# A decoder trunk with mLSTM, differential attention and grouped experts on one core: negated attention scores, maps mixed in one operation, pinned additions

## The chip, the cores and the metric

The kernel runs on one core of a Trainium2 chip. The metric is the device time in microseconds (us). Five engines work from queues of their own, each in order: TensorE (PE in the profile; PEld its weight loads), VectorE (DVE), ScalarE (ACT), GpSimd (POOL) and SyncE (SP), which issues nearly all transfers. Time before: 1250.63 us, median of 3 runs (1246.63 to 1251.24).

## The reference, cut to what matters

512 tokens of 1024 channels pass two layers. Each has a token mixer and then 16 experts in 4 groups, two experts for a token. Layer 0 mixes by an mLSTM, layer 1 by differential attention, which the change touches:

```python
q = _partial_rope(_rms(q, q_norm), positions)      # 8 heads, 2 maps each, 64 dims
k = _partial_rope(_rms(k, k_norm), positions)
q = jnp.transpose(q, (0, 2, 3, 1, 4)) * (B_HEAD_DIM ** -0.5)     # 1/8
...
    sc = jnp.einsum('bhcqd,bhckd->bhcqk', q[:, :, :, s0:e], k[:, :, :, :e])
    mask = (s0 + jnp.arange(Q_BLOCK))[:, None] >= jnp.arange(e)[None, :]
    p = jax.nn.softmax(jnp.where(mask, sc, -jnp.inf), axis=-1)
    a = p[:, :, 0] - lam * p[:, :, 1]
    outs.append(jnp.einsum('bhqk,bhkv->bhqv', a, v[:, :, :e]))
```

## The kernel before, in words

Tokens are worked in four tiles of 128 rows; `xt[t]` keeps tile t of the residual in SBUF through both layers. A layer is a mixer, an output projection, a routing and an expert stage. Large weights come by SP transfers into a few raw buffers (`load`, L212), and are split into a high and a low part: ScalarE copies the high part (L224), VectorE or GpSimd subtracts it (L225); TensorE then makes three products for one.

The order of instructions is not all written by hand. `later` and `step` (L89, L98) put small pieces of work between the products of a projection, so many steps after they become possible. Then a scheduler of the framework sets each engine's final order by its own estimate, except where `ordered` (keep in program order) or `issue_after` binds it.

*Attention, layer 1.* The projection of q, k and v runs in four groups of two heads. `evac_qk` (L839) normalises and rotates a tile of q or k on VectorE, with the reciprocal root on GpSimd (L326), and turns it by TensorE into `qTb` or `kTb`, where the copy on ScalarE scales each channel by `wcq` or `wck` (L863). `scores` (L867) treats one query tile j of one head h; there are 4 x 8 of these, of 128, 256, 384 or 512 columns. For each of its two maps TensorE multiplies (L876), VectorE adds the mask, writes the result to SBUF and reduces its maximum (L879), VectorE scales that maximum by -1/8 (L882), and ScalarE takes the exponential with it as bias and sums the row (L883). Then VectorE takes the reciprocals of both sums (L886), forms the second map's factor (L887), multiplies the second map by it (L888) and adds it to the first (L889). `probs_T` and `values` turn the mixed map and multiply it by v. Beside this the modulation of later stages is computed: ScalarE scales weight rows (L255) and GpSimd accumulates them (L256).

*From layer 0 to layer 1.* The last expert of layer 0 adds its result to the residual out of PSUM banks, two halves for each of the four token tiles (L1575). Layer 1 begins with `normed_T` (L329): for each tile the sum of squares on ScalarE (L332), its scaling on VectorE (L325, the tile `r`), the root on GpSimd, and turning on TensorE.

*Experts.* The experts' weights, 6 transfers of 1 MB for each expert, are prefetched into slots (`Prefetch`, L1238), of which some are buffers that attention used; a slot comes free when the product that reads it is done.

Of the kernel before, what the change touches and what calls it, by code (L numbers as in the profile page):

```python
# [15 lines left out]
AF = mybir.ActivationFunctionType  # L16
ALU = mybir.AluOpType
# [4 lines left out]
P = 128  # L22
S = 512
D = 1024
# [3 lines left out]
NEG = -1e30  # L28
# [32 lines left out]
def trunk(ctx, tc, x, c, positions, norm1, norm2, w_ada, b_ada, a_w_in, a_b_if, a_h_norm, a_w_out,  # L61
# [145 lines left out]
        G.iota(slot, pattern=[[1, P]], base=0, channel_multiplier=0, **ints)  # L207


    loads, last, act_last = [], [], []  # L210

    def load(src, a, n, name, where=None, after=None):  # L212
        pool, tag, bufs = where or (raws, "raw", N_RAW)
# [115 lines left out]
    def normed_T(l, t, pool, junk, dst, rows, bank):  # L329

        ss = small.tile([P, 1], F32, tag="ss", name=f"ss{l}{t}", bufs=4)
        A.activation(junk, xt[t], AF.Square, accum_out=ss)  # L332
        r = rstd_of(ss, 1, D, f"r{l}{t}")
        ps = [bank(f"hT{l}{t}{hf}") for hf in range(2)]
        for kt in range(NK):
            T.transpose(ps[kt // 4][:, kt % 4 * P:(kt % 4 + 1) * P], xt[t][:, kt * P:(kt + 1) * P], ident)
        row = rows[t // 2][:, t % 2 * P:(t % 2 + 1) * P]
        T.transpose(row, r.to_broadcast([P, P]), ident)
        rrow = pool.tile([P, P], F32, tag="rot", name=f"rrows{l}{t}", bufs=2)
        A.activation(rrow, row, AF.Copy)  # L340
        for hf in range(2):
            V.tensor_tensor(dst[:, hf * 4:hf * 4 + 4], ps[hf].rearrange("p (k t) -> p k t", k=4),
                            rrow[:, None, :].to_broadcast([P, 4, P]), op=ALU.mult)
# [425 lines left out]
    def attention_constants(pool):  # L769
# [17 lines left out]
        for nm, w in (("q", b_q_norm), ("k", b_k_norm)):  # L787
            wr = pool.tile([P, R2], F32, name=f"wr{nm}")
            hold(wr[:, 0:1])
            SP.dma_start(wr, w[0:1, 0:R2].to_broadcast([P, R2]))  # L790
            wc = const.tile([P, 1], F32, name=f"wc{nm}")
            hold(wc)
            V.memset(wc, 1.0)
            for c0 in (0, BHD):
                SP.dma_start(wc[c0 + R2:c0 + BHD], w[0:1, R2:].rearrange("o d -> d o"))
            tab = const.tile([P, NT, 2 * R2], F32, name=f"tab{nm}")
            bc = lambda a: a[:, None, :].to_broadcast([P, NT, ROPE_HALF])
            V.tensor_tensor(tab[:, :, 0:8], cos, bc(wr[:, 0:8]), op=ALU.mult)
            V.tensor_tensor(tab[:, :, 8:16], cos, bc(wr[:, 8:16]), op=ALU.mult)
            V.tensor_tensor(tab[:, :, 24:32], sin, bc(wr[:, 0:8]), op=ALU.mult)  # L800
            V.tensor_tensor(tab[:, :, 16:24], sin, bc(wr[:, 8:16]), op=ALU.mult)
            V.tensor_scalar(tab[:, :, 16:24], tab[:, :, 16:24], -1.0, None, op0=ALU.mult)
            tabs.append(tab)
            wcol.append(wc)
        att.extend((nlam, onr))

    def attention(outer, mods):
# [4 lines left out]
        with ExitStack() as st:  # L812
# [10 lines left out]
            maskW = pool.tile([P, S], F32, name="maskW")  # L823
            G.memset(maskW[:, 0:S - P], 0.0)
            past(maskW[:, S - P:])
            V.tensor_scalar(maskW[:, S - P:], maskW[:, S - P:], 0.0, NEG, op0=ALU.is_gt, op1=ALU.mult)
            a1 = scale_of(1, slice(0, 4)) + scale_of(1, slice(4, 8))
            rows = [y_tile(f"rrow1{i}") for i in range(2)]
            for t in range(NT):
# [37 lines left out]
            def scores(j, h):  # L867
                take("mx", 4)
                take("p0", 3)
                n = (j + 1) * P  # L870
                pr = []
                mx = pool.tile([P, 6], F32, tag="mx", name=f"mx{j}{h}", bufs=4)
                for cc in range(2):
                    q0 = cc * BHD
                    ps = y_tile(f"s{j}{h}{cc}")
                    T.matmul(ps[:, 0:n], part(qTs, h)[q0:q0 + BHD, j * P:(j + 1) * P], part(kTs, h)[q0:q0 + BHD, 0:n],  # L876
                             start=True, stop=True)
                    p = pool.tile([P, S], F32, tag=f"p{cc}", name=f"p{j}{h}{cc}", bufs=3)
                    V.tensor_tensor_reduce(p[:, 0:n], ps[:, 0:n], maskW[:, S - n:S], scale=1.0, scalar=NEG,  # L879
                                           op0=ALU.add, op1=ALU.max, accum_out=mx[:, cc:cc + 1])  # L880
                    pr.append(p)
                    V.tensor_scalar(mx[:, cc:cc + 1], mx[:, cc:cc + 1], -0.125, None, op0=ALU.mult)  # L882
                    A.activation(p[:, 0:n], p[:, 0:n], AF.Exp, scale=0.125, bias=mx[:, cc:cc + 1],  # L883
                                 accum_out=mx[:, 2 + cc:3 + cc])
                p0, p1 = pr
                V.reciprocal(mx[:, 4:6], mx[:, 2:4])  # L886
                V.scalar_tensor_tensor(mx[:, 5:6], mx[:, 5:6], mx[:, 2:3], nlam, op0=ALU.mult, op1=ALU.mult)  # L887
                V.tensor_scalar(p1[:, 0:n], p1[:, 0:n], mx[:, 5:6], None, op0=ALU.mult)  # L888
                V.tensor_tensor(p0[:, 0:n], p0[:, 0:n], p1[:, 0:n], op=ALU.add)  # L889
                later(5, lambda: probs_T(j, h, p0, mx))  # L890

            def probs_T(j, h, p0, mx):
# [369 lines left out]
    def moe(l, pool, grow, fetch, by_rank, xgs, lst, lstd, ids, gates, rows2, twins, count, exc, past, pk, eid):  # L1262
# [269 lines left out]
        for e in range(NE):  # L1532
# [32 lines left out]
            if e == NE - 1:  # L1565
                mine = weighted_few(py, e), mine
                for t in range(NT):
# [4 lines left out]
                    to_tokens(banks[t], t, *mine, False, True)  # L1572
                    for hf in range(2):
                        x = xt[t][:, hf * 512:(hf + 1) * 512]
                        V.tensor_tensor(x, x, banks[t][hf], op=ALU.add)  # L1575
            elif e >= NE - NSEL:
                selected.append((weighted_few(py, e), places(e)))
            elif e == NE - NSEL - 1:
# [91 lines left out]
```

## Time and profile before

| | |
|---|---|
| time, median of 3 runs | 1250.63 us |
| the profiled execution: its time | 1244.82 us |
| its span, first to last instruction | 1243.0 us |
| TensorE busy | 1128.2 us, 91% |
| VectorE busy | 855.2 us, 69% |
| ScalarE busy | 686.7 us, 55% |
| GpSimd busy | 378.7 us, 30% |
| granted TensorE clock, mean of the span | 0.939 of full speed |
| chain that ended last, by engine | PE 63%, DVE 18%, DMA 10%, ACT 3%, issue 2%, POOL 2% |

A row of the profile names the line, the engine, the operation, the tile written and those read, the shapes, the count, the busy time and the mean of one in ns, then the idle time of the engine just before it and what ended that. The chain is followed back from the last instruction, at each step to what released it. In a timeline a row begins with its start and its length in us; a row with a count merges instructions that follow each other.

### The profile page before, as it was taken

To read this page: it belongs to the slowest core of one execution; us is meant where nothing else is said; L and a number is where in the kernel's file an instruction comes from. 1 tells how busy PE (TensorE), PEld (TensorE's weight loads), DVE (VectorE), ACT (ScalarE), POOL (GpSimd) and SP (SyncE) were. 2 spreads that over 40 slices of the span, in tenths; PEclk is the share of its full clock that TensorE was granted. 3 is DMA by queue.
4 is the path that set the end of the run, shared out by engine and by line. 5 is a ranking of instruction groups with operands and counts; after the bars stand their busy time and mean duration, and the time that the engine had idled before them with its cause. 6 is when DMAs were issued, how large, how long until landed. Compare 5 with 4: busy or idle time off the path is not lost.

```text
span 1243.0 us, 17100 instructions
## 1 busy us (share of the span) xinstructions
PE 1128.2 (91%) x5826; PEld 824.4 (66%) x5826; DVE 855.2 (69%) x1608; ACT 686.7 (55%) x1146; POOL 378.7 (30%) x273
## 2 busy tenths in 40 slices
PE   6999999997999999977889889988897999999976
PEld 3677777776787774323888768766576787774322
DVE  4566878887899892035867788985767898893024
ACT  3456675443788883104666557655553788883100
POOL 2555481543211111103441554642233211101100
PEclk8999999996999999999899899897796999999998
DMA  9788661284899999996332434310365899999994
GB/s 349 253 287 306 243 209 72 115 325 180 305 388 392 378 382 378 396 413 239 103 136 69 136 113 159 136 69 14 156 269 186 294 390 377 383 379 367 395 413 168
DMA packets 104170, 320.78 MB, mean 258 GB/s; under 512 B 12673, under 2 KB 25097, under 8 KB 103056
## 3 DMA queue, kind: packets, MB, share of 16 engines
q1 hardware_dynamic: 95120, 298.67, 64.8%
q0 software_dynamic: 8960, 20.99, 4.7%
q8 instruction: 47, 0.77, 0.2%
q14 instruction: 43, 0.35, 0.1%
HBM read 309.66 MB, written 20.97 MB: 266 GB/s over the span
## 4 chain that ended last, share of the span: by engine, by line
PE 63%; DVE 18%; DMA 10%; ACT 3%; issue 2%; POOL 2%; SPq 0%; DVEq 0%; POOLq 0%; ACTq 0%
PE pge L233 8%; PE pue L233 8%; PE pge L1298 7%; PE po L233 6%; PE py0e L233 4%; DMA ada<-in_w_ada_dram 4%; PE py1e L233 4%; DMA we<-in_moe_w_gu_dram 3%; PE pye L1325 3%; PE s L876 2%; DMA b00w<-in_b_w_in_dram 2%; PE xTe L386 1%; PE o L908 1%; DVE qrow L856 1%; PE pcf L1357 1%
## 5 line engine op out<-in xcount | busy, mean ns | idle before, releaser
L256 POOL TENSOR_TENSOR acc<-acc,ada 128x1024 f32<-128x1024 f32 x58 | 152.0, 2621 | 68.6 <-ACT ada L255 30.6
L1298 PE MATMUL pge<-we,xfe 128*64 128x512 f32 x448 | 106.9, 619 | 19.3 <-DMA we<-in_moe_w_gu_dram 19.3
L1270 POOL DMA_INDIRECT xg<-h2d,lstd x26 | 26.5, 1018 | 225.1 <-PE xTe L386 154.5
L1307 DVE TENSOR_TENSOR acte<-acte,pge 128x256 f32<-128x256 f32 x14 | 5.9, 421 | 119.9 <-ACT acte L1306 119.9
L255 ACT ACTIVATE ada<-ada,cact 128x1024 f32<-128x1024 f32 x58 | 64.7, 1145 | 37.3 <-DMA ada<-in_w_ada_dram 37.2
L1298 PEld LDWEIGHTS pge<-we,xfe 128*64 128x64 f32 x448 | 30.5, 141 | 74.8 <-issue 51.4
L326 POOL TENSOR_TENSOR qrs<-qrs,nhalf 128x4 f32<-128x4 f32 x32 | 36.0, 1129 | 81.7 <-DVE qrs L325 62.5
L883 ACT ACTIVATE p<-p,mx 128x128 f32<-128x128 f32 (+3 forms) x64 | 35.5, 556 | 44.1 <-DVE mx L882 44.1
L1325 PE MATMUL pye<-we,aTe 128*64 128x512 f32 x224 | 50.8, 594 | 1.7 <-ACT aTe L1314 1.1
L876 PE MATMUL s<-kTb,qTb 64*128 64x128 f32 (+3 forms) x128 | 44.2, 536 | 7.9 <-DVE mx L879 7.0
L471 POOL TENSOR_TENSOR wo<-wo,grow 128x1024 f32<-128x1024 f32 x16 | 40.1, 2524 | 29.7 <-DVE wos102l L225 14.9
L1306 ACT ACTIVATE acte<-pge 128x256 f32<-128x256 f32 x14 | 5.4, 384 | 74.9 <-PE pge L1298 74.9
L1325 PEld LDWEIGHTS pye<-we,aTe 128*64 128x64 f32 x224 | 15.9, 137 | 33.6 <-issue 30.0
L879 DVE CUSTOM_DVE_ANT_0 p<-s,maskW 128x128 f32<-128x128 f32 (+3 forms) x64 | 29.8, 485 | 10.1 <-PE s L876 7.2
L1422 POOL DMA_INDIRECT yd<-yoe,lstd x12 | 14.7, 1224 | 52.3 <-ACT yoe L1517 51.7
L326 POOL TENSOR_TENSOR ors<-ors,nhalf 128x2 f32<-128x2 f32 (+1 forms) x12 | 11.9, 998 | 56.3 <-DVE ors L325 28.2
L908 PE MATMUL o<-vb,aTs 128*128 128x128 f32 x160 | 27.2, 308 | 1.5 <-ACT o L937 0.8
L386 PE MATMUL xTe<-ident,xg 128*128 128x128 f32 x144 | 23.0, 290 | 5.8 <-POOL we L216 3.3
L1338 POOL DMA_INDIRECT yd<-yo,rows x8 | 8.0, 1001 | 65.7 <-ACT yo L1337 65.4
L908 PEld LDWEIGHTS o<-vb,aTs 128*128 128x128 f32 x160 | 23.8, 217 | 6.2 <-ACT aTs L900 1.9
L1337 ACT ACTIVATE yo<-pye,twins 128x512 f32<-128x512 f32 x8 | 5.5, 687 | 38.9 <-PE pye L1325 38.9
L876 PEld LDWEIGHTS s<-kTb,qTb 64*128 64x128 f32 x128 | 16.0, 203 | 16.2 <-DVE mx L879 8.6
(2546 smaller groups left out, 3932.8 us busy)
## 6 DMA issues: line engine op xcount, KB each, us to landing
we<-in_moe_w_gu_dram SPq DMA_DIRECT2D x128, 1024.0 KB, 8.8
we<-in_moe_w_down_dram SPq DMA_DIRECT2D x64, 1024.0 KB, 8.8
ada<-in_w_ada_dram SPq DMA_DIRECT2D x48, 1024.0 KB, 5.5
we<-yd SPq DMA_DIRECT2D x8, 1024.0 KB, 18.3
wo<-in_a_w_out_dram SPq DMA_DIRECT2D x4, 1024.0 KB, 5.0
wo<-in_b_w_out_dram SPq DMA_DIRECT2D x4, 1024.0 KB, 4.9
x<-in_x_dram SPq DMA_DIRECT2D x4, 512.0 KB, 4.6
qk0w<-in_a_w_in_dram SPq DMA_DIRECT2D x2, 1024.0 KB, 15.4
```

Of the source, the lines that this page charges most:

```text
L233: T.matmul(ps, (xh, xh, xl)[i], w, start=first and i == 0, stop=last and i == 2)
L255: A.activation(raw[:, k], raw[:, k], AF.Copy, scale=cact[:, kt:kt + 1])
L256: G.tensor_tensor(acc, acc, raw[:, k], op=ALU.add)
L326: pows.append(G.tensor_tensor(r, r, nhalf[:, 0:ncol], op=ALU.pow))
L386: T.transpose(ps[:, k * P:(k + 1) * P], row[:, kt * P:(kt + 1) * P], ident)
L471: G.tensor_tensor(raw[:, k], raw[:, k], grow, op=ALU.mult)
L876: T.matmul(ps[:, 0:n], part(qTs, h)[q0:q0 + BHD, j * P:(j + 1) * P], part(kTs, h)[q0:q0 + BHD, 0:n], start=True, stop=True)
L879: V.tensor_tensor_reduce(p[:, 0:n], ps[:, 0:n], maskW[:, S - n:S], scale=1.0, scalar=NEG, op0=ALU.add, op1=ALU.max, accum_out=mx[:, cc:cc ...
L883: A.activation(p[:, 0:n], p[:, 0:n], AF.Exp, scale=0.125, bias=mx[:, cc:cc + 1], accum_out=mx[:, 2 + cc:3 + cc])
L908: T.matmul(po[:, 0:P], aT[:, kb * P:(kb + 1) * P], part(vs, h)[:, kb * P:(kb + 1) * P], start=kb == 0, stop=kb == j)
L1298: T.matmul(pgu[hf * CS:(hf + 1) * CS].rearrange("p (g c) -> p g c", g=2), x[:, kt], w[:, :, hf], start=kt == 0, stop=kt == NK - 1))
L1325: T.matmul(py[hf * CS:(hf + 1) * CS], aT[:, k, ch * CS:(ch + 1) * CS], w[:, 0, hf * 512:(hf + 1) * 512], start=ch + k == 0, stop=ch + k == 2))
```

## The change

q is scaled by -1/8 through `wcq`, once, so that the score products come out as the negated, scaled scores; the mask's constant changes its sign; the reduction takes the minimum, which is the bias of the exponential as it stands, and the exponential has the scale -1. L882 goes. The two operations that mix the maps become one. The last additions of a layer are kept in program order, and in layer 1 the scaling `r` of tiles 2 and 3 is issued after the last of layer 0's additions.

```diff
@@ normed_T
-        r = rstd_of(ss, 1, D, f"r{l}{t}")
+        with tc.issue_after(added[0].ins) if added and t > 1 else nullcontext():
+            r = rstd_of(ss, 1, D, f"r{l}{t}")
@@ attention_constants
+            if nm == "q":
+                V.tensor_scalar(wc, wc, -0.125, None, op0=ALU.mult)
@@ attention
-            V.tensor_scalar(maskW[:, S - P:], maskW[:, S - P:], 0.0, NEG, op0=ALU.is_gt, op1=ALU.mult)
+            V.tensor_scalar(maskW[:, S - P:], maskW[:, S - P:], 0.0, -NEG, op0=ALU.is_gt, op1=ALU.mult)
@@ scores
-                    V.tensor_tensor_reduce(p[:, 0:n], ps[:, 0:n], maskW[:, S - n:S], scale=1.0, scalar=NEG,
-                                           op0=ALU.add, op1=ALU.max, accum_out=mx[:, cc:cc + 1])
+                    V.tensor_tensor_reduce(p[:, 0:n], ps[:, 0:n], maskW[:, S - n:S], scale=1.0, scalar=-NEG,
+                                           op0=ALU.add, op1=ALU.min, accum_out=mx[:, cc:cc + 1])
                     pr.append(p)
-                    V.tensor_scalar(mx[:, cc:cc + 1], mx[:, cc:cc + 1], -0.125, None, op0=ALU.mult)
-                    A.activation(p[:, 0:n], p[:, 0:n], AF.Exp, scale=0.125, bias=mx[:, cc:cc + 1],
+                    A.activation(p[:, 0:n], p[:, 0:n], AF.Exp, scale=-1.0, bias=mx[:, cc:cc + 1],
                                  accum_out=mx[:, 2 + cc:3 + cc])
...
-                V.tensor_scalar(p1[:, 0:n], p1[:, 0:n], mx[:, 5:6], None, op0=ALU.mult)
-                V.tensor_tensor(p0[:, 0:n], p0[:, 0:n], p1[:, 0:n], op=ALU.add)
+                V.scalar_tensor_tensor(p0[:, 0:n], p1[:, 0:n], mx[:, 5:6], p0[:, 0:n], op0=ALU.mult, op1=ALU.add)
@@ moe, the last expert
-                        V.tensor_tensor(x, x, banks[t][hf], op=ALU.add)
+                        added[:] = [V.tensor_tensor(x, x, banks[t][hf], op=ALU.add)]
+                        ordered(added[0])
```

The scheduler works on the whole program, so the order moves at other places too. Two of them matter. The first is VectorE where layer 0 ends, before (x0 to x3 are the token tiles, pcf the banks, r10 to r13 the scalings of layer 1's tiles 0 to 3):

```order
L1575 TENSOR_TENSOR x1_83<-x1_83,pcf11_5042 128x512
L325 TENSOR_SCALAR r10_5134<-ss10_5132 128x1
L325 TENSOR_SCALAR r11_5168<-ss11_5166 128x1
L1575 TENSOR_TENSOR x2_86<-x2_86,pcf20_5075 128x512
L1575 TENSOR_TENSOR x2_86<-x2_86,pcf21_5076 128x512
L325 TENSOR_SCALAR r12_5202<-ss12_5200 128x1
L1575 TENSOR_TENSOR x3_89<-x3_89,pcf30_5085 128x512
L1575 TENSOR_TENSOR x3_89<-x3_89,pcf31_5086 128x512
```

and the same place on VectorE with the change:

```order
L1576 TENSOR_TENSOR x1_83<-x1_83,pcf11_5043 128x512
L325 TENSOR_SCALAR r10_5135<-ss10_5133 128x1
L325 TENSOR_SCALAR r11_5169<-ss11_5167 128x1
L1576 TENSOR_TENSOR x2_86<-x2_86,pcf20_5076 128x512
L1576 TENSOR_TENSOR x2_86<-x2_86,pcf21_5077 128x512
L1576 TENSOR_TENSOR x3_89<-x3_89,pcf30_5086 128x512
L1576 TENSOR_TENSOR x3_89<-x3_89,pcf31_5087 128x512
L325 TENSOR_SCALAR r12_5203<-ss12_5201 128x1
```

The two additions of tile 3 moved ahead of r12. The second is VectorE at head 0, query tile 3, before (p300 and p301 are the two maps, mx30 their column values, qrow and rot belong to the rotation of k):

```order
L879 ISA p301_6267,mx30_6258<-s301_6265,maskW_5118 128x512
L879 ISA mx30_6258 128x1
L855 TENSOR_TENSOR qrow_6202<-qrow_6202,tabk_907 128x4x16
L882 TENSOR_SCALAR mx30_6258<-mx30_6258 128x1
L856 TENSOR_TENSOR qrow_6202<-qrow_6202,rot_6212 128x4x16
L886 RECIPROCAL mx30_6258<-mx30_6258 128x2
L887 SCALAR_TENSOR_TENSOR mx30_6258<-mx30_6258,nlam_873 128x1
L888 TENSOR_SCALAR p301_6267<-p301_6267,mx30_6258 128x512
L889 TENSOR_TENSOR p300_6261<-p300_6261,p301_6267 128x512
```

and VectorE with the change, where the reductions are L882 and the reciprocal is L888:

```order
L882 ISA p301_6249,mx30_6241<-s301_6247,maskW_5119 128x512
L882 ISA mx30_6241 128x1
L888 RECIPROCAL mx30_6241<-mx30_6241 128x2
L889 SCALAR_TENSOR_TENSOR mx30_6241<-mx30_6241,nlam_873 128x1
L890 SCALAR_TENSOR_TENSOR p300_6244<-p301_6249,mx30_6241,p300_6244 128x512
```

The two pieces of rotation moved out from between the reduction and the reciprocal, and the scaling and the multiplication are gone. A reciprocal that has nothing but the reduction's own read-out ahead of it (L882 of the old kernel not counted) stands at 3 of the 32 heads before and at 6 with the change. SP's order is the same in both kernels. On TensorE, ScalarE and GpSimd rows change places within layer 1's beginning, its attention and its output projection, with the same instructions in sum.

## Rows read from the trace of the kernel before

**Rows 1.** The page's first line: span and instructions of the whole execution.

```profile
span 1243.0 us, 17100 instructions
```

**Rows 2.** Stretches: length, busy us (count) of PE, PEld, DVE, ACT, POOL; PEclk, DMA, GB/s.

```profile
636.00:690.00 54.00, 54.00 (x392) 46.42 (x391) 38.68 (x141) 36.74 (x94) 14.44 (x11) 1.00 0.23 79
690.00:760.00 70.00, 60.08 (x405) 50.69 (x403) 59.92 (x134) 42.68 (x102) 42.39 (x21) 0.93 0.44 151
760.00:810.00 50.00, 45.16 (x302) 38.96 (x301) 43.49 (x124) 34.10 (x87) 27.16 (x17) 0.90 0.38 126
810.00:853.00 43.00, 32.80 (x190) 25.47 (x191) 32.18 (x95) 24.75 (x65) 12.72 (x9) 0.83 0.13 50
853.00:900.00 47.00, 42.98 (x189) 31.10 (x187) 33.91 (x81) 23.39 (x65) 17.37 (x9) 0.83 0.29 112
```

**Rows 3.** Chain of waits from 640 to 900 us, shares by line.

```profile
by line: PE s L876 10.0%; issue 5.1%; DVE qrow L856 4.8%; PE o L908 4.2%; DVE p L879 4.1%; PE po L233 4.0%; DVE p L889 3.4%; DVE mod L273 3.4%; DVE qrow L850 3.1%; DVE mx L887 2.5%; DVE p L888 2.3%; PE qkT L862 2.0%; DVE orow L923 1.8%; DVE
```

**Rows 4.** Timeline of all engines from 697 to 705 us.

```profile
697.75 2.49 DVE L888 TENSOR_SCALAR p<-p,mx 128x512 f32<-128x512 f32 x1
...
700.02 5.17 POOL L256 TENSOR_TENSOR acc<-acc,ada 128x1024 f32<-128x1024 f32 x2
700.27 2.71 DVE L889 TENSOR_TENSOR p<-p,p 128x512 f32<-128x512 f32 x1
...
703.32 0.26 DVE L882 TENSOR_SCALAR mx<-mx 128x1 f32<-128x1 f32 x2
...
704.41 0.17 DVE L886 RECIPROCAL mx<-mx 128x2 f32<-128x2 f32 x1 [0.82 <-ACT p L883]
```

**Rows 5.** Groups by line and shape: count | busy us, mean ns | idle before, releaser.

```profile
L882 DVE TENSOR_SCALAR mx<-mx 128x1 f32<-128x1 f32 x64 | 8.5, 146 | 0.2
...
L888 DVE TENSOR_SCALAR p<-p,mx 128x512 f32<-128x512 f32 x8 | 5.9, 734 | 0.2
L888 DVE TENSOR_SCALAR p<-p,mx 128x384 f32<-128x384 f32 x8 | 3.3, 418 | 0.2
L888 DVE TENSOR_SCALAR p<-p,mx 128x256 f32<-128x256 f32 x8 | 2.8, 352 | 0.2
L888 DVE TENSOR_SCALAR p<-p,mx 128x128 f32<-128x128 f32 x8 | 2.3, 283 | 0.2
...
L253 DVE SCALAR_TENSOR_TENSOR acc<-ada,cact,acc 128x1024 f32<-128x1024 f32 x12 | 15.4, 1281 | 11.3 <-DMA ada<-in_w_ada_dram 6.7 <-POOL acc L256 4.6
...
L225 DVE TENSOR_TENSOR b14s0l<-b14w,b14s0h 128x1024 fp32r<-128x1024 f32 x1 | 1.2, 1226 | 3.1 <-ACT b14s0h L224 3.1
...
L879 DVE CUSTOM_DVE_ANT_0 p<-s,maskW 128x512 f32<-128x512 f32 x16 | 10.8, 685 | 3.0 <-PE s L876 2.9
...
L879 DVE CUSTOM_DVE_ANT_0 p<-s,maskW 128x128 f32<-128x128 f32 x16 | 4.1, 283 | 0.9 <-PE s L876 0.7 <-ACT orow L910 0.2
...
L886 DVE RECIPROCAL mx<-mx 128x2 f32<-128x2 f32 x32 | 5.1, 161 | 7.1 <-ACT p L883 6.9
```

**Rows 6.** Timeline where layer 0 ends: start us, us, engine, what.

```profile
573.41 7.14 PE L1357 MATMUL pcf<-yo,self 64*128 64x512 f32 x32 [0.85 <-DVE yo L1331]
...
578.40 1.27 DVE L1575 TENSOR_TENSOR x<-x,pcf 128x512 f32<-128x512 f32 x2
...
581.24 1.15 ACT L255 ACTIVATE ada<-ada,cact 128x1024 f32<-128x1024 f32 x1 [2.94 <-DMA ada<-in_w_ada_dram]
...
583.46 0.15 DVE L325 TENSOR_SCALAR r<-ss 128x1 f32<-128x1 f32 x1 [3.78 <-ACT sq L332]
583.54 1.29 DVE L1575 TENSOR_TENSOR x<-x,pcf 128x512 f32<-128x512 f32 x2
...
584.92 1.06 ACT L332 ACTIVATE sq<-x 128x1024 f32<-128x1024 f32 x1 [1.49 <-DVE x L1575]
```

**Rows 7.** Layer 1's experts: from the timeline of SP, then from the chain.

```profile
938.39 33.84 SPq L218 DMA_DIRECT2D we<-in_moe_w_gu_dram  x4
...
1195.23 20.07 DMA we<-in_moe_w_gu_dram
```

More of the change, by code (lines that the diff above doesn't have):

```diff
@@ L207, in moe_constants @@
         G.iota(slot, pattern=[[1, P]], base=0, channel_multiplier=0, **ints)
-    loads, last, act_last = [], [], []
+    loads, last, act_last, added = [], [], [], []
     def load(src, a, n, name, where=None, after=None):
```

## The prediction

> **What bounds the kernel now.** I read the whole span first, then the stretch in which the edited lines run, then that stretch's chain of waits, then the timeline and the groups of single lines. The profiled execution spans 1243.0 us [rows 1]. The scores, exponentials and mixing of the two maps run in layer 1, from about 640 to 900 us; the additions that are pinned matter at about 575 to 587 us, where layer 0 hands over to layer 1.
>
> The stretch table [rows 2] shows two regimes. From 636 to 690 us TensorE is busy 54.00 of 54.00 us at full clock, and VectorE only 38.68: there a shorter VectorE list buys nothing. From 690 to 853 us VectorE is busy 59.92, 43.49 and 32.18 us of 70, 50 and 43, while TensorE falls to 60.08, 45.16 and 32.80, at a granted clock of 0.93, 0.90 and 0.83 of full speed. Neither is saturated; they wait for one another. From 853 to 900 us it is the same in weaker form.
>
> The chain of waits from 640 to 900 us [rows 3] says how much of an edited line decides the end: the multiplication of the second map (L888) holds 2.3% of 260 us, 6.0 us, the addition of the maps (L889) 3.4%, 8.8 us. L882, the scaling of the maximum, is not among the lines named, the smallest of which holds 1.8%.
>
> The timeline shows why such small operations are on the chain [rows 4]. GpSimd runs accumulations of 2.6 us each (the row at 700.02 holds two), and VectorE operations with operands in SBUF stretch beside them: the 512-column L888 takes 2.49 us and the L889 behind it 2.71. Without a stretch L888 has 283 ns for 128 columns, and 352 for 256 [rows 5].
>
> **The change part by part.**
>
> *The negated scores.* 64 instructions of L882 go. They are busy 8.5 us in sum, 146 ns each, two in a row 0.26 us [rows 4, 5]. Each stands between a reduction and its exponential, so it also delays ScalarE. From the chain the bounds are 0 and 4.7 us (1.8% of 260, the smallest line named) [rows 3]. I take 2.0: it is small work, but in the direct path. The reduction by minimum replaces one by maximum on the same operands; the exponential has another constant scale. Both keep their shapes and counts, and I cost them at nothing. One operation on a 128x1 constant is added, in layer 0's shadow: at most the 0.15 us of an L882, taken as 0.
>
> *The mixing in one operation.* 32 multiplications (L888) go: 5.9 + 3.3 + 2.8 + 2.3 = 14.3 us busy [rows 5]. The 32 additions become operations that multiply by a column and add, of the same width. I take their price as that of the additions: such an operation on 1024 columns, both tensors f32 in SBUF (L253), takes 1281 ns, and a plain subtraction of 1024 columns (L225) 1226 [rows 5]. So what is gained is L888 alone: upper end 14.3, lower end 0 where something else is late, and by the chain 6.0 (42% of 14.3). I take 6.0, since it is read from the stretch itself. Late next where L888 goes are the reciprocal's wait for the exponentials and TensorE's own queue.
>
> [...]
>
> *What moves with it.* With L882 gone, the new order puts the reciprocal directly behind the second reduction in 6 of 32 heads, against 3 before (L882 not counted). VectorE works in order and then idles for the exponentials; one such wait is 0.82 us [rows 4], and all of them now are 6.9 us [rows 5]. Three more cost 2.5 us of VectorE, 42% of it on the path as for L888: +1.0 us. Behind the waiting reciprocal stand the next head's reductions, and behind those TensorE's score products, which need a freed bank. Some TensorE products, POOL accumulations and ScalarE rows change places in this stretch; SP's queue doesn't change. I set no price on that: it has no sign, and the range carries it.
>
> *The pinned additions.* Now the last two additions of layer 0 (token tile 3) stand behind the r of tile 2, which waits for a square on ScalarE that itself stands behind a weight product that waits for a DMA until 581.24. So VectorE, free at 579.67, sits idle until 583.46 and adds tile 3 at 583.54, though TensorE's last bank was written at 573.41 + 7.14 = 580.55 [rows 6]. Pinned ahead, these additions run at about 580.6. The square of tile 3 then needn't wait its 1.49 us before 584.92 [rows 6], and the rows of r copied behind it on ScalarE come as much earlier. The square of tile 2 is not touched: it still waits for the DMA. Gain 1.5, with bounds 0 (the following VectorE work meets a GpSimd accumulation at another moment) and 1.5. The r of tile 2 now waits for the tile 3 additions, at nothing: they end some 1.5 us before its square does. At the end of layer 1 the order is already the pinned one, so nothing comes from there.
>
> *Does it reach the end?* In layer 1's expert stage the weights' transfers set the end: the chain has a weight transfer of 20.07 us at 1195.23, and the queue's last four prefetches wait 33.84 us from 938.39 for slots that only the experts free [rows 7]. So that stream's restart moves with the end of attention, and I carry the gain through one to one.
>
> Sum: 2.0 + 6.0 - 1.0 + 1.5 = 8.5 us. The profiled execution took 1244.82 us, so it would take 1236.3. It lies 5.8 us under the median of the three runs, 1250.63; the same 8.5 us off the median give **1242.1**, 0.7% faster. About 0.5% is what a measurement of this kernel can tell from no change, that is 6.3 us: 1244.4 and 1256.9.
>
> **The rivals.**
>
> *Full relief.* If VectorE alone paces 690 to 900 us, all of L888, and L882 at 4.7, come off, with 2.5 lost to the reciprocals: 14.3 + 4.7 - 2.5 + 1.5 = 18.0, so 1232.6. For it: TensorE's granted clock of 0.83 to 0.93 there, which is low where it has waited. Against: 636 to 690 us can give nothing, and the chain has less than half of L888. Chance 0.17.
>
> *Hidden behind TensorE.* The edits do what they say on VectorE, but the products' own queue is late next, and only the pin and a rest of about 1.5 us remain: 3.0, so 1247.6. For it: TensorE busy 138 of 163 us from 690 to 853. Against: the clock in the same rows. Chance 0.23.
>
> *The mixing at half rate.* [...] Chance 0.05.
>
> *Slower: VectorE's queue stands behind the exponentials.* Each reciprocal that follows its reductions directly stops VectorE for 0.82 us, and with it the next reductions, the score banks and TensorE. Were all 32 heads so placed, 26.2 us of waiting would stand where 6.9 are now: 19.3 more. Fully on the path against 9.5 gained by the rest, that is 9.8 us lost: 1260.4. It decides from 12 more heads on (9.5 / 0.82). For it: a VectorE list without L882 has nothing else to put in between. Against: the order has three more, not twelve. Chance 0.10.
>
> **How the numbers follow.** The forecast keeps 0.45; its own range is 4 to 12 us of gain, 1238 to 1247, by other meetings with GpSimd and the new places on TensorE. Faster by over 0.5% are about four fifths of it and the full relief: 0.36 + 0.17 = 0.53. Slower by over 0.5%: 0.10, and 0.02 for new places that fall badly. The rest, 0.35, is within 0.5%. The range, 1231 to 1251, takes in the forecast, full relief, the hidden case and the half rate, and leaves out the slower one and a tail of the full relief.
>
> **What would show it.** Right: VectorE's busy time from layer 1's scores to their end about 20 us less; the mixing at about what a reduction of its width takes, 0.28 to 0.69 us [rows 5], where it isn't stretched; tile 3's additions right behind tile 2's, with ScalarE's two squares back to back; the reciprocals' wait at about 9 us; TensorE's granted clock from 690 to 853 us higher. Wrong: mixing rows of over 1 us for 512 columns with no GpSimd accumulation beside them (half rate); a reciprocals' wait over 16 us (slower); VectorE that much less busy with TensorE's stretch as long as before (hidden); or a gain that is there when experts of layer 1 begin but not at the end (the transfers hold it).

## The result, and the profile after

| | before | changed |
|---|---|---|
| median of 10 runs each, same batch | 1251.45 us (1246.63 to 1256.41) | 1238.80 us (1235.36 to 1243.24) |
| the profiled execution: its time | 1244.82 us | 1238.19 us |
| its mean granted clock | 0.939 | 0.940 |

The ratio is 0.9895, with a 95% interval of 0.9874 to 0.9917: 13.1 us faster (10.4 to 15.8). The forecast was 8.5 us. The two profiled executions, however, differ by 6.6 us only: the one of the kernel before, 1244.82 us, lies below all ten others. Both figures have to be explained.

The first line of the changed kernel's page, against [rows 1]:

```profile
span 1236.4 us, 17003 instructions
```

The stretch table of the changed kernel, in the stretches of [rows 2] moved 6 us ahead (the same columns):

```profile
630.00:684.00 54.00, 54.00 (x399) 47.45 (x398) 35.91 (x125) 37.52 (x90) 15.98 (x11) 1.00 0.29 98
684.00:754.00 70.00, 64.43 (x424) 55.19 (x424) 57.83 (x120) 44.96 (x110) 40.13 (x22) 0.93 0.41 136
754.00:804.00 50.00, 45.28 (x318) 38.30 (x318) 42.77 (x102) 33.14 (x87) 29.57 (x18) 0.97 0.43 148
804.00:847.00 43.00, 34.63 (x190) 26.48 (x191) 30.16 (x82) 24.86 (x66) 13.13 (x9) 0.78 0.14 50
847.00:894.00 47.00, 42.62 (x190) 32.12 (x190) 30.70 (x64) 24.16 (x67) 17.25 (x9) 0.84 0.29 112
```

TensorE is fuller where it had waited most: 64.43 us of 70 against 60.08, 34.63 of 43 against 32.80. VectorE is a little emptier in each row. The granted clock in these rows is 0.78 to 1.00 of full speed; it is lowest in the row in which TensorE is idle longest, 8.37 us.

To see where the time came from I cut both traces at the same work instead: from the first projection product of the second group's q (`b02p`) to the first of the third group's v (`bv4p`), from there to the first of the fourth group's v (`bv6p`), and on to the end of the last value product. First the kernel before:

```profile
639.40:736.50 97.10, 90.50 (x646) 77.85 (x645) 73.18 (x231) 64.19 (x159) 37.83 (x24) 0.96 0.32 109
736.50:807.50 71.00, 63.27 (x409) 53.00 (x407) 63.39 (x156) 45.05 (x113) 40.78 (x23) 0.90 0.44 149
807.50:903.70 96.20, 80.62 (x412) 60.68 (x412) 69.92 (x186) 51.57 (x140) 32.85 (x20) 0.84 0.20 77
```

and the changed kernel between the same points:

```profile
638.60:736.40 97.80, 93.62 (x645) 79.97 (x644) 70.59 (x192) 64.02 (x159) 35.97 (x22) 0.97 0.32 108
736.40:800.10 63.70, 59.41 (x408) 50.54 (x406) 56.14 (x134) 42.55 (x112) 40.22 (x24) 0.95 0.46 155
800.10:897.00 96.90, 81.86 (x412) 62.41 (x412) 65.83 (x153) 53.37 (x142) 34.87 (x21) 0.82 0.22 84
```

The whole gain of attention in this pair lies in the middle row, 71.0 to 63.7 us, where GpSimd is busiest and VectorE had been busy 63.39 of 71.00. The outer rows are each 0.7 us longer than before, though VectorE lost 2.6 and 4.1 us in them.

The chain of waits of the changed kernel from 638 to 894 us, shares by line, against [rows 3]:

```profile
by line: PE s L879 8.6%; issue 5.0%; PE o L909 3.8%; DVE mx L889 3.8%; PE po L233 3.6%; DVE orow L924 3.4%; DVE qrow L853 3.2%; DVE p L882 3.1%; DVE p L890 2.6%; DVE qrow L858 2.2%; DMA b16w<-in_b_w_in_dram 2.1%; DVE rot L856 2.0%; DVE mod 
```

The two mixing lines held 3.4% and 2.3%, 14.8 us of 260; the one that replaces them (L890) holds 2.6% of 256, 6.7 us. But the factor, a column of one element, rose from 2.5% to 3.8%, and the normalisation of the output rows (L923, now L924) from 1.8% to 3.4%. Part of the time was handed on. The groups say to what. First the rows of the kernel before that [rows 5] doesn't have:

```profile
L887 DVE SCALAR_TENSOR_TENSOR mx<-mx,nlam 128x1 f32<-128x1 f32 x32 | 13.3, 416 | 0.6
...
L889 DVE TENSOR_TENSOR p<-p,p 128x256 f32<-128x256 f32 x8 | 3.4, 422 | 0.1
...
L923 DVE TENSOR_TENSOR orow<-orow,ors 128x512 f32<-128x512 f32 x4 | 2.7, 684 | 0.0
...
L889 DVE TENSOR_TENSOR p<-p,p 128x128 f32<-128x128 f32 x8 | 2.3, 288 | 0.1
```

and the changed kernel:

```profile
L853 DVE TENSOR_TENSOR qrow<-qrow,qrs 128x256 f32<-128x256 f32 x32 | 22.7, 710 | 4.2 <-POOL qrs L326 4.1
L889 DVE SCALAR_TENSOR_TENSOR mx<-mx,nlam 128x1 f32<-128x1 f32 x32 | 14.4, 449 | 0.7
L882 DVE CUSTOM_DVE_ANT_0 p<-s,maskW 128x512 f32<-128x512 f32 x16 | 10.9, 687 | 7.2 <-PE s L879 5.5 <-ACT orow L911 1.6
...
L890 DVE SCALAR_TENSOR_TENSOR p<-p,mx,p 128x512 f32<-128x512 f32 x8 | 8.1, 1019 | 0.2
...
L924 DVE TENSOR_TENSOR orow<-orow,ors 128x512 f32<-128x512 f32 x4 | 6.0, 1500 | 0.0
...
L888 DVE RECIPROCAL mx<-mx 128x2 f32<-128x2 f32 x32 | 5.1, 160 | 7.0 <-ACT p L885 6.6
L890 DVE SCALAR_TENSOR_TENSOR p<-p,mx,p 128x384 f32<-128x384 f32 x8 | 4.9, 615 | 0.1
L890 DVE SCALAR_TENSOR_TENSOR p<-p,mx,p 128x256 f32<-128x256 f32 x8 | 3.9, 483 | 0.2
L890 DVE SCALAR_TENSOR_TENSOR p<-p,mx,p 128x128 f32<-128x128 f32 x8 | 2.8, 348 | 0.2
```

The mixing costs 348, 483 and 615 ns for 128, 256 and 384 columns: 1.04 ns a column, as the addition alone did (288 and 422 ns), and 60 ns more for each operation. The reciprocals' wait for the exponentials is 6.6 us. The reductions of 512 columns wait longer than before, 7.2 against 3.0 us, and mostly for TensorE. L924's four wide rows take 1500 ns on the mean, where they took 684: two of them meet an accumulation and take 1.79 and 2.84 us, and the two others take 0.68 us as before.

What holds VectorE is seen in the changed kernel's timeline near 782 us, VectorE and GpSimd alone:

```profile
781.49 7.47 POOL L256 TENSOR_TENSOR acc<-acc,ada 128x1024 f32<-128x1024 f32 x3 [0.94 <-ACT acc L251]
...
781.67 2.38 DVE L273 TENSOR_TENSOR mod<-cs,vcol 128x8 f32<-128x8 f32 x1
783.97 0.21 DVE L859 TENSOR_TENSOR qrow<-qrow,rot 128x64 f32<-128x64 f32 x1
784.11 0.41 DVE L882 CUSTOM_DVE_ANT_0 p<-s,maskW 128x256 f32<-128x256 f32 x1
...
784.45 2.07 DVE L856 TENSOR_TENSOR rot<-qrow,tabq 128x32 f32<-128x32 f32 x1
...
786.66 2.38 DVE L858 TENSOR_TENSOR qrow<-qrow,tabq 128x64 f32<-128x64 f32 x1
```

Three accumulations, of 2.37 to 2.53 us, run with under 0.1 us between them, and beside each one some VectorE operation is held until it ends, be it of 8, 32 or 64 columns: the accumulations end at 784.02, 786.48 and 788.95 us, the held operations at 784.05, 786.52 and 789.04. The reduction at 784.11, which reads PSUM and SBUF, takes its usual 0.41 (418 ns on the mean of its 16), though the second accumulation starts at 784.10.

The hand-over from layer 0, against [rows 6]:

```profile
579.95 1.28 DVE L1576 TENSOR_TENSOR x<-x,pcf 128x512 f32<-128x512 f32 x2 [0.91 <-PE pcf L1358]
...
580.69 1.15 ACT L255 ACTIVATE ada<-ada,cact 128x1024 f32<-128x1024 f32 x1 [3.04 <-POOL maskW L136]
...
581.75 1.04 ACT L332 ACTIVATE sq<-x 128x1024 f32<-128x1024 f32 x1
...
582.92 1.06 ACT L332 ACTIVATE sq<-x 128x1024 f32<-128x1024 f32 x1
582.92 0.15 DVE L325 TENSOR_SCALAR r<-ss 128x1 f32<-128x1 f32 x1 [1.69 <-ACT sq L332]
```

Tile 3's additions run at 579.95 instead of 583.54, and ScalarE's two squares follow each other without a wait. From the last bank of layer 0 to the first projection product it is 9.38 us instead of 10.75.

And SP's queue in the experts, against [rows 7], from its timeline:

```profile
931.70 34.28 SPq L218 DMA_DIRECT2D we<-in_moe_w_gu_dram  x4
```

It waits about as long as before (33.84 us), from a moment 6.7 us earlier.

| us from the span's start | before | changed | e6_later | e11_before_later |
|---|---|---|---|---|
| first projection product of layer 1 | 591.30 | 589.30 | 587.41 | 587.57 |
| end of the last value product | 903.72 | 896.98 | 894.17 | 899.99 |
| first product of layer 1's experts | 960.59 | 954.51 | 946.88 | 952.79 |
| end | 1243.03 | 1236.40 | 1229.01 | 1235.16 |

### The profile page after: what moved, and what is told of

Read it like the earlier page. It is cut to its first block, busy times and chain, and to the rows that moved or that the text cites. A ratio compares the mean times of both kernels' runs of the same rounds, so it can differ in the third digit from the quotient of the medians.

```text
span 1236.4 us, 17003 instructions
## 1 busy us (share of the span) xinstructions
PE 1127.3 (91%) x5826; PEld 826.3 (67%) x5826; DVE 843.0 (68%) x1513; ACT 685.6 (55%) x1146; POOL 378.4 (31%) x273
## 4 chain that ended last, share of the span: by engine, by line
PE 63%; DVE 16%; DMA 11%; ACT 5%; POOL 3%; issue 2%; SPq 0%; POOLq 0%; DVEq 0%; ACTq 0%
PE pge L233 8%; PE pue L233 8%; PE pge L1299 6%; PE po L233 6%; DMA we<-in_moe_w_gu_dram 5%; DMA ada<-in_w_ada_dram 4%; PE py0e L233 4%; PE py1e L233 4%; PE pye L1326 3%; POOL acc L256 2%; PE s L879 2%; PE pcf L1358 2%; PE xTe L387 1%; ACT ada L255 1%; PE o L909 1%
## 5 line engine op out<-in xcount | busy, mean ns | idle before, releaser
L472 POOL TENSOR_TENSOR wo<-wo,grow 128x1024 f32<-128x1024 f32 x16 | 40.1, 2526 | 33.0 <-DVE wos102l L225 14.3
L882 DVE CUSTOM_DVE_ANT_0 p<-s,maskW 128x128 f32<-128x128 f32 (+3 forms) x64 | 30.0, 485 | 14.4 <-PE s L879 9.7
L909 PEld LDWEIGHTS o<-vb,aTs 128*128 128x128 f32 x160 | 23.5, 212 | 7.7 <-ACT aTs L901 2.1
L326 POOL TENSOR_TENSOR ors<-ors,nhalf 128x2 f32<-128x2 f32 (+1 forms) x12 | 10.8, 901 | 54.4 <-DVE ors L325 42.1
```

Source lines behind the costliest of these rows:

```text
L326: pows.append(G.tensor_tensor(r, r, nhalf[:, 0:ncol], op=ALU.pow))
L472: G.tensor_tensor(raw[:, k], raw[:, k], grow, op=ALU.mult)
L909: T.matmul(po[:, 0:P], aT[:, kb * P:(kb + 1) * P], part(vs, h)[:, kb * P:(kb + 1) * P], start=kb == 0, stop=kb == j)
```

## The experiments

The theory of the prediction, called A below, is that each operation taken away gives the share of it that lay on the path. The main rival, B, is that the new order of the whole list decides, since the scheduler deals VectorE's operations and GpSimd's accumulations out anew for every edit. C is the hand-over, D that VectorE alone paces, E that TensorE's granted clock differs between executions. In us, a ratio is taken of the median before in the same batch: 1249.2 for e1 to e4, 1249.0 for e5 to e8, 1249.1 for e9 to e12. The ratio is not the quotient of the two medians, and the two can differ by 2 or 3 us: by the medians e2_neg gains 8.8 us, and e9_small and e10_wide lose 1.4 and 1.2. The diffs show the lines that matter.

**e1_pin: the pinned additions alone.**

```diff
+        with tc.issue_after(added[0].ins) if added and t > 1 else nullcontext():
+            r = rstd_of(ss, 1, D, f"r{l}{t}")
...
+                        ordered(added[0])
```

> Only the additions are pinned; attention is as before. Theory A (each part gives what it takes off the path): 1.5 us faster than before, all of it between 578 and 587 us, ratio 0.999. Theory B (the new order of instructions, not the work removed, makes the gain): anything from 4 us faster to 4 us slower, since this kernel's attention stage is scheduled anew. Theory C (most of the whole gain of 12.7 us comes from where layer 0 meets layer 1): over 4 us faster.

Measured: 1245.77 us, ratio 0.9981 (0.9956 to 1.0007), 2.4 us, which the runs can't tell from nothing. The trace can: the hand-over takes 8.88 us instead of 10.75, and attention behind it is as long as before (264.2 us against 264.3, from the first `b02p` to the last value product). In all five traces of kernels with the pin the hand-over takes 8.5 to 9.4 us (mean 8.9), in the nine without it 9.9 to 10.9 (mean 10.4). So the pin is worth what was forecast, and C, a gain that comes mostly from there, falls.

**e2_neg: the negated scores alone.**

```diff
-                    V.tensor_scalar(mx[:, cc:cc + 1], mx[:, cc:cc + 1], -0.125, None, op0=ALU.mult)
```

> Only the scores are negated, so that L882 goes; the maps are mixed in two operations, nothing is pinned. Theory A: 2 us faster, ratio 0.998. Theory D (VectorE paces attention, so what it is spared comes off in full and its waits with it): 4.7 to 8.5 us faster, ratio 0.993 to 0.996. Theory B: no fixed sign.

Measured: 1240.45 us, ratio 0.9947 (0.9926 to 0.9969): 6.6 us for 64 operations on one column, three times the term of the forecast. Attention takes 258.5 us.

**e3_mix: the mixing in one operation alone.**

```diff
-                V.tensor_scalar(p1[:, 0:n], p1[:, 0:n], mx[:, 5:6], None, op0=ALU.mult)
-                V.tensor_tensor(p0[:, 0:n], p0[:, 0:n], p1[:, 0:n], op=ALU.add)
+                V.scalar_tensor_tensor(p0[:, 0:n], p1[:, 0:n], mx[:, 5:6], p0[:, 0:n], op0=ALU.mult, op1=ALU.add)
```

> Only the maps are mixed in one operation; L882 stays, nothing is pinned. Theory A: 6.0 us less 2.0 for the operation's 61 ns over a plain addition at 32 heads, so 4 to 6 us faster, ratio 0.995 to 0.997. Theory D: 12 us faster, ratio 0.990. Theory B: no fixed sign.

Measured: 1237.68 us, ratio 0.9922 (0.9890 to 0.9953), 9.7 us. In its profiled execution attention takes 252.9 us at a granted clock of 0.946 there, against 264.3 at 0.903. TensorE is busy for 225.9 us of it, against 234.4 before, with the same products: 8.5 of the 11.4 us lie there, beside the higher clock, and not in waits.

**e4_neg_mix: both, without the pin** (the two diffs above).

> Both changes of attention without the pin. If the parts add up (A or D): the sum of the two single runs, and 1.5 us slower than the whole change, about 11 us faster than before, ratio 0.991. Theory B: it differs from that sum by over 4 us. Theory C: under 9 us faster.

Measured: 1239.91 us, ratio 0.9944 (0.9923 to 0.9965). Both together give 7.0 us, no more than either alone; 16.3 would be their sum. Attention takes 258.3 us, the same as in the changed kernel (258.4). Added prices (theory A in its plain form) fall here. Its median and the change's, 1238.80, are closer than the two ratios, each of which is taken in its own batch.

**e5_before: the kernel before again,** with no edit.

> The kernel before, unchanged, profiled a second time; ratio 1.000. The first profiled execution of before took 1244.8 us, under its median of about 1250. Theory E (TensorE's granted clock in attention makes the difference between executions): the span comes out at 1246 to 1252 us, with the granted clock from the second projection group to the last value product under the 0.903 of the first one and TensorE busy over 235 us there. Rival (the transfers of layer 0 make it): the attention stretch within 1 us of 264.3 again, and layer 0 longer.

Measured: 0.9999 (0.9967 to 1.0031), and a profiled span of 1243.0 us again, at a clock of 0.937. Attention takes 263.3 us, at 0.903 again. So it shows how far two profiles of one kernel agree, 1.0 us here, and decides nothing about E.

**e6_later: the change, with the reciprocals and the mixing put off by one step of the work list.**

```diff
-                p0, p1 = pr
+                later(1, lambda: mixed(j, h, *pr, mx))
+
+            def mixed(j, h, p0, p1, mx):
...
-                later(5, lambda: probs_T(j, h, p0, mx))
+                later(4, lambda: probs_T(j, h, p0, mx))
```

> The whole change, and the reciprocal, the factor and the mixing of each head are put off by one step of the work list, so that other work of VectorE stands between them and the reductions. If the in-order wait of the reciprocal for the exponentials (6.6 us in the profile of the change) is on the path: 3 to 6 us faster than the change, ratio to before 0.985 to 0.987. If it is covered: as the change, 0.990. If one more step of delay makes TensorE wait for the mixed maps at the end of a group: 2 to 5 us slower than the change, 0.992 to 0.994.

Measured: 1227.90 us, ratio 0.9815 (0.9783 to 0.9848). It beats both kernels, by 23.1 us and by about 10 (against e7_dose, which equals the change, in the same batch). But not by the wait that it was aimed at. The groups of e6_later show the reciprocals waiting as long as before, and the factor taking 661 ns on the mean, where it took 449 in the change:

```profile
L892 DVE SCALAR_TENSOR_TENSOR mx<-mx,nlam 128x1 f32<-128x1 f32 x32 | 21.1, 661 | 0.7
...
L891 DVE RECIPROCAL mx<-mx 128x2 f32<-128x2 f32 x32 | 5.1, 160 | 7.1 <-ACT p L885 6.7
```

What moved is the output projection behind attention. Its products of this layer begin at 832.1 us instead of 846.6, between the last heads, and from the last value product to the experts' first product it takes 52.7 us instead of 57.5 (table above). Of the 7.4 us between the two profiled ends 4.8 lie there; 1.9 lie before layer 1's first projection product.

**e7_dose: the change, with 32 multiplications of the second map put back** (by 1.0).

```diff
+                V.tensor_scalar(p1[:, 0:n], p1[:, 0:n], 1.0, None, op0=ALU.mult)
```

> The whole change, and for each head the second map is multiplied by 1.0 in place before the mixing: an operation of the shape of the old L888 comes back (14.3 us of VectorE). Theory A: 6 us slower than the change, ratio to before 0.995. Theory D: 12 to 14 us slower than the change, ratio 1.000. Theory B: no relation to the work put back, 0.988 to 0.992 or over 1.002.

Measured: 1238.09 us, ratio 0.9911 (0.9880 to 0.9941), the same as the change. Its groups show where part of the added work goes:

```profile
L888 DVE RECIPROCAL mx<-mx 128x2 f32<-128x2 f32 x32 | 5.1, 160 | 4.3 <-ACT p L885 3.9
...
L890 DVE TENSOR_SCALAR p<-p 128x256 f32<-128x256 f32 x8 | 4.4, 546 | 0.4 <-ACT p L885 0.4
L890 DVE TENSOR_SCALAR p<-p 128x512 f32<-128x512 f32 x8 | 3.3, 409 | 0.0
L890 DVE TENSOR_SCALAR p<-p 128x384 f32<-128x384 f32 x8 | 2.7, 337 | 0.0
...
L890 DVE TENSOR_SCALAR p<-p 128x128 f32<-128x128 f32 x8 | 1.7, 208 | 0.0
```

The sum of its stretches from the first `b02p` to the last value product, to set beside 258.40 us, TensorE 234.89 and VectorE 192.56 in the changed kernel:

```profile
sum 257.90, PE 233.00 PEld 190.69 DVE 197.15 ACT 160.55 POOL 111.92; mean PE 77.67 PEld 63.56 DVE 65.72 ACT 53.52 POOL 37.31
```

The rows of the 32 added operations last 12.1 us, but VectorE is busy 4.6 us longer only, in part because rows overlap. Its idle time falls by 5.1 us, 2.7 of them from the reciprocals' wait. The granted clock in this stretch is 0.927, against 0.908 in the changed kernel, and TensorE is busy 1.9 us less; so that it is free at an equal clock too is not shown. D, by which it would cost 12 to 14 us, falls.

**e8_mix_pin: the change with L882 kept** (diffs of e1_pin and e3_mix).

> The mixing in one operation and the pin, L882 stays. If parts add up (A, D): slower than the whole change by what L882 is worth, 2 to 6 us, ratio to before 0.992 to 0.994. Theory B, after the run with the mixing alone was ahead of the run with both attention edits (0.9922 against 0.9944): the order without L882 takes back what its work saves, and this kernel is as fast as the whole change or up to 5 us faster, 0.986 to 0.990.

Measured: 1237.69 us, ratio 0.9902 (0.9867 to 0.9937). The negated scores add nothing that shows once the other two parts are in; with six runs, 2 or 3 us would not show.

**e9_small: the kernel before, with L882 doubled.**

```diff
+                    V.tensor_scalar(mx[:, cc:cc + 1], mx[:, cc:cc + 1], 1.0, None, op0=ALU.mult)
```

> The kernel before with the scaling of the maximum doubled: 64 more operations on 128x1, each a multiplication by 1.0 behind L882, 146 ns each, 8.5 us of VectorE in sum. This is the negated scores' saving turned round. Theory A (each operation has its own price on the path; taking L882 away alone gave 0.53%): 6 to 7 us slower, ratio about 1.005, with ScalarE's wait for the reductions about 6 us longer. Theory B (what an edit gives is decided by the new order of the whole list, and not by the work): anything within 8 us on either side, of no fixed sign. The forecast's own term (2.0 us for 64 such operations) would make it 1.0016, that is no difference that can be measured.

Measured: 1250.54 us, ratio 1.0036 (1.0017 to 1.0055), 4.5 us slower (2.1 to 6.9). The timeline of e9_small shows what one costs VectorE's list, L882 being the old and L883 the added one:

```profile
836.49 0.27 DVE L882 TENSOR_SCALAR mx<-mx 128x1 f32<-128x1 f32 x2
836.67 0.27 DVE L883 TENSOR_SCALAR mx<-mx 128x1 f32<-128x1 f32 x2
```

Rows overlap: two of them last 0.27 us, but the next begins after 0.18. So 64 take 5.8 us of the list here, not the 8.5 us of their busy time. The sum of its stretches from the first `b02p` to the last value product, against 264.30 us, TensorE 234.39 and VectorE 206.49 before:

```profile
sum 268.30, PE 239.73 PEld 194.61 DVE 210.64 ACT 160.12 POOL 109.92; mean PE 79.91 PEld 64.87 DVE 70.21 ACT 53.37 POOL 36.64
```

Attention is 4.0 us longer. The length is all in TensorE's busy time, at a granted clock of 0.892 there against 0.903; its idle time is no longer than before (28.6 us against 29.9).

**e10_wide: the kernel before, with the multiplication of the second map doubled.**

```diff
+                V.tensor_scalar(p1[:, 0:n], p1[:, 0:n], 1.0, None, op0=ALU.mult)
```

> The kernel before with the multiplication of the second map doubled: 32 more operations of 128 to 512 columns (by 1.0, in place, ahead of L888), 14.3 us of VectorE in sum. The mixing's saving turned round. Theory A: as much slower as the mixing alone was faster, 0.78%, about 10 us; the forecast's own term says 6.0 us, ratio 1.005. Theory B: not slower in proportion, within 5 us of the kernel before or even faster, as in the change itself, where the same 32 operations put back cost nothing.

Measured: 1250.35 us, ratio 1.0038 (1.0015 to 1.0061), 4.7 us slower (1.9 to 7.6). In its trace attention, on the same terms, is 4.7 us longer:

```profile
sum 269.00, PE 238.64 PEld 193.87 DVE 208.88 ACT 160.04 POOL 114.65; mean PE 79.55 PEld 64.62 DVE 69.63 ACT 53.35 POOL 38.22
```

In the kernel before the added work costs something near the 6.0 us of the forecast; in the changed kernel, e7_dose, it costs nothing that shows. Again TensorE's busy time carries it (238.64 against 234.39 us, clock 0.892).

**e11_before_later: the kernel before, nothing removed, the mixing put off as in e6_later.**

> The kernel before, with nothing removed, and the reciprocals, the factor and the two mixing operations put off by one step of the work list (the turning keeps its place). If putting off is worth the same 0.8% without the change as on top of it (theory B: the place of these operations in VectorE's list counts, not their sum), the ratio is about 0.992 and the time near that of the change. If it only pays once L882 and L888 are gone (theory A, with the reciprocal's wait as what is late next), it is within 0.4% of the kernel before.

Measured: 1240.72 us, ratio 0.9954 (0.9927 to 0.9980), 5.7 us. From the last value product to the experts it takes 52.8 us against 56.9, as in e6_later. So the putting off earns in the same place with and without the change. That is 4.1 of the 7.9 us between the two profiled ends; 3.7 lie before layer 1's first projection product (table above), whose lines this edit does not touch.

**e12_sooner: the kernel before, the same instructions, the turning one step sooner.**

```diff
-                later(5, lambda: probs_T(j, h, p0, mx))
+                later(4, lambda: probs_T(j, h, p0, mx))
```

> A control of how far a new order alone moves the time: the kernel before with the turning of the mixed map put on the work list four steps on instead of five, the same instructions. Theory B: a difference of several us, of either sign, of the size of the single parts' differences (0.2 to 0.8%). Theory A: nothing over 0.3%, since no work is added or taken away, and the mixed map is ready well before.

Measured: 1243.59 us, ratio 0.9973 (0.9947 to 0.9998). A new order with the same work is worth 0.27% here, and in e11 0.46%. Single edits of this kernel can't be priced more finely than that by undoing them one at a time.

**Attention in all fourteen traces** tells the work from the order better than the times do. Taken from the first `b02p` to the last value product, it lasts 261.4 to 264.3 us in the five traces with all of the work (before, e1, e5, e11, e12), 252.9 to 258.7 in the seven that spare some (the change, e2, e3, e4, e6, e7, e8), and 268.2 and 269.1 in the two that add some (e9, e10). The groups don't meet. It isn't the clock alone either: at a granted clock of 0.908 to 0.909 there, e11 takes 263.1 us, and the change, e4 and e6 take 258.4, 258.3 and 258.7. So the work sets the sign in attention, against B in its plain form; but how much is spared doesn't set the size, against A.

**What the clock adds** needs no run of its own. Each execution has its mean granted clock on record. Of the kernel before 86 executions came with e1 to e12: mean 1248.4 us, clock 0.929 to 0.946 of full speed, mean 0.9355. Time and clock go together (correlation -0.82): 0.96 us less for each 0.001. An estimate from 1128.2 us of TensorE work, all of it longer by 0.001 of 0.9355, is near that, 1.2 us. The 15 executions at 0.939 to 0.941 took 1243.4 us on the mean, and the one that was profiled, at 0.939, took 1244.82. The changed kernel's ten executions are all at 0.939 to 0.942, mean 0.9401; the nine up to 0.941 took 1239.2. So at an equal clock the change is worth 4.2 us between means and 6.6 between the two profiles, and the clock, 0.0046 higher, about 4.4 more (an estimate, 0.96 x 4.6). That makes 8.6 of the 13.1 us. By the fitted line instead of the 15 executions the first part is 5.2 and the sum 9.5; the remaining 3.6 us are there because the kernel before, in the batch of the result, took 1251.9 us on the mean, 3.6 over these 86, and the clocks of those ten executions are not on record.

The edits that take work away have mean clocks of 0.9399 to 0.9442, those with equal or more work 0.9349 to 0.9382 (e9_small 0.9360, e10_wide 0.9362). Against the fitted line, that is at an equal clock, e2, e3 and e4 are 3.6, 4.5 and 2.7 us faster, but e1, e12 and e11, which take no work away, are 3.6, 3.1 and 5.1 faster as well, and e9 and e10 2.6 and 3.1 slower. So in the whole time, at an equal clock, the sparing edits can't be told from a mere new order (e6_later, 12.7 us faster, apart); what marks them is the higher clock that came with them. That it is the clock that makes the time, and not a common cause of both, is argued, not shown.

## Why the prediction was right, and where it was not

The sign and the range held, and the time, 1238.8 us, is 3.3 us under the forecast of 1242.1. The gain is half as much again as forecast. The mechanism, VectorE work taken off attention and a hand-over relieved, is the right one, but that the number came so near is in part luck: one term was too small, the terms don't add up, and a higher clock, which was in no term, came with some 4 us. Step by step:

- **L882, taken as 2.0 us of bounds 0 and 4.7.** Mis-sized, as far as single runs show. Doubling it costs 4.5 us (2.1 to 6.9), leaving it out gives 6.6 (3.9 to 9.2); the signs agree, though a new order alone gave 3.4 and 5.7. That it isn't among the chain's named lines said little; a likely reason, not shown, is that a short operation between a reduction and its exponential delays what comes behind it without being named. Its busy time was the wrong measure too, in the other direction: 8.5 us busy are 5.8 of the list where e9_small's timeline shows it.
- **L888, taken as 6.0 of 14.3 us.** Not contradicted: 4.7 us (1.9 to 7.6) when doubled, 9.7 (5.9 to 13.7) when merged; but nothing when put back in the changed order (e7_dose). The price of the merged operation was 61 ns over an addition's (483 ns for 256 columns, where L889 took 422 in the kernel before), 2 us in 32 that the forecast took at nothing, a small miss.
- **The mixing at half rate, 0.05.** Fell. No run shows it: the merged operation takes 348, 483 and 615 ns for 128, 256 and 384 columns, 1.04 ns a column, and the reductions' step in the kernel before was 1.05 ((685 - 283) ns over 384 columns [rows 5]). Seven of its eight rows of 512 columns take 0.74 to 0.75 us, under the 1 us that was named as the sign; the eighth, 2.92 us, has a GpSimd row beside it.
- **The reciprocals' new waits, -1.0.** Fell. The order did put three more directly behind their reductions, and those cost what was forecast: the six idle for 4.8 us, where the three idled for 2.4. But the other 26 idle for 2.3 us, where the other 29 idled for 4.6, so the wait for the exponentials went from 6.9 to 6.6 us [rows 5]. The prediction priced the new waits and took the old ones as fixed. Why the others fell is not shown; the reductions come later, waiting for TensorE's scores, so an earlier exponential may be further on by then. The rival built on this wait, slower by 9.8 us, did not come.
- **The pin, 1.5.** Held: 1.37 us in the changed kernel's trace, 1.87 in e1_pin's, and no overlap between the hand-overs of the traces with it and without it. In the pair, though, the stretch from there to `b02p` is 1.2 us longer than before (49.3 against 48.1), so little of it is left where attention begins.
- **Through to the end one to one.** Held: 6.1 us at the experts' first product, 6.6 at the end.
- **The sum of terms.** Failed as a method. The parts alone give 2.4, 6.6 and 9.7 us, two together 7.0, all three 13.1. Added up they are 18.7. (That the two attention edits don't add up is clear of noise; the same of the three parts against the whole, which ran in another batch, is not.) e7_dose and e8_mix_pin show single parts worth nothing that can be told on top of the rest. Two reasons are in the traces. First, the prediction added up the times of rows that overlap. The rows of attention last 20.9 us less in sum (237.5 to 216.6), near the 20 that were expected, but VectorE's busy time fell by 13.9 only (206.49 to 192.56, the sums of the three rows cut at the same work); of the 9.4 us that the rows of L882 last there, only 2.6 are covered by no other VectorE row. Second, the stretches beside GpSimd stay when the work goes. With the same 22 accumulations, 27 VectorE operations lose 54.4 us to them before, 28 lose 53.8 with the change, 27 lose 52.8 in e7_dose. (Lost is what a row takes over the fastest tenth of its kind in all fourteen traces, counted where that is over 0.7 us.) In the end 5.9 of the 13.9 us shorten attention, and VectorE idles for 8 us more.
- **The same 8.5 us off the median as off the profiled execution.** Failed. The profiled execution of the kernel before stood at a clock of 0.939, its mean execution at 0.9355. The pair of profiles, at 0.939 and 0.940, gained 6.6 us, a little under the forecast; the medians differ by 12.7, with a higher clock beside it. The prediction named a higher clock from 690 to 853 us as a sign, and gave it no price. In the pair itself the sign is faint: 0.93, 0.97 and 0.78 against 0.93, 0.90 and 0.83 [rows 2].

Full relief (1232.6) did not come, though e6_later shows that there was more to be had, in another place. Hidden behind TensorE (1247.6) did not come either: TensorE's idle time in attention, the three rows' length less its busy time, fell from 29.9 to 23.5 us.

What stays open is how much of the 13.1 us belongs to the particular order, and whether the higher clock is what the spared work brings about or only comes with it. A shift of the order alone gave 3.4 us (e12_sooner, 0.2 to 6.6) and 5.7 (e11_before_later, 2.5 to 9.1), and no run held the order fixed while taking work away. The whole change was timed in one batch only; in the later ones e4_neg_mix, e7_dose and e8_mix_pin gained 7.0, 11.1 and 12.2 us.

## What to carry to other kernels

Where a scheduler deals the order out anew, price an edit by adding the same work as well as by removing it, and run one control with equal work and another order: a difference below that control's is not shown to be the edit's. Cut the traces at the same work as well, since a stretch that holds the edit tells more than the end does. The time that VectorE lost beside GpSimd accumulations wasn't saved here when stretched operations went: others were held in their place, and the loss stayed between 52.8 and 54.4 us. Don't add up rows that overlap. And compare a profiled execution with others at its own granted clock before its difference is put on the median.

## What the runs showed that was not expected

A VectorE operation on a single column, the factor, took 0.20 to 0.22 us at 28 of the 32 heads before, and 2.32 at 739.58 us, beside an accumulation of GpSimd; on the mean 416 ns before and 661 in e6_later. The operations of 8, 32 and 64 columns in the timeline near 782 us were held alike, for 2.1 to 2.4 us, so their place mattered there and not their size. A multiplication by a constant took 208 and 337 ns for 128 and 384 columns where the one by a column of SBUF took 283 and 418 [rows 5]. And putting three or four instructions of each head off by one step took 4 to 5 us out of a stage that doesn't contain them, the output projection, which could begin earlier among the last heads.
